# Forgetting heads scored in pairs with the decay summed into the scores, and the relative-position masks moved into the output projection

## The chip, the cores and the metric

The kernel runs on one core of one Trainium2 chip. The metric is the device time of one execution in microseconds (us). Five engines work side by side and wait for each other through semaphores: TensorE (PE in the rows; its weight loads are PEld), VectorE (DVE), ScalarE (ACT), GpSimd (POOL) and SyncE (SP), which issues the transfers from HBM.

## The reference, cut to what matters

Two transformer blocks run one after the other on 256 tokens of width 1024. The change lies in the mixer of the first block. It has three parts side by side: a gated part, six forgetting heads and four heads over a memory of 256 rows. Their outputs are joined and projected by `w_out`.

```
c = jnp.cumsum(log_f, axis=1).transpose(0, 2, 1)
for i in range(S // Q_BLOCK):                 # two blocks of 128 queries
    s = einsum('bhtd,bhsd->bhts', q[block i], k[keys up to the block's end]) * scale
    s = s + c[:, :, start:end, None] - c[:, :, None, :end]
    s = jnp.where(mask, s, NEG_INF)
    p = jax.nn.softmax(s, axis=-1)
    outs.append(einsum('bhts,bhsd->bthd', p, v))
...
y = jnp.concatenate([out_a, out_b, out_c], axis=-1) @ w_out[l]
```

A softmax row doesn't change when one number is added to all of it, so the term of the query, `c[start:end]`, may be left out of `s`; the term of the key may not.

The first attention of the second block adds a bias that depends on the distance of two positions through 32 buckets. The kernel builds it from masks: for each pair of positions, and for each bucket, whether the distance is at or above the bucket's threshold.

## The kernel before, in words

Activations stand with the features on the partitions, two halves of 128 tokens. Weights come from HBM in `raw` tiles; each tile is cut into chunks of up to 1024 columns, and each chunk is split into a high part `wh` (ScalarE, L103) and a low part `wl` (VectorE, L113), so that a product in three passes (high x high, low x high, high x low) keeps float32 precision. `Stream.get` hands out the next chunk and starts the split of the chunk four further on; a low part is issued when the following chunk is split, or by `ws.low()`. The last low part of a `raw` tile lets SP issue the next transfer.

The order on each engine is the order of the code: nothing is moved by a scheduler. `Pipe` interleaves the attention heads with the dense products. Each `step()` scores a head ahead, transposes the probabilities of the head two steps back (L321), runs the masks and the maximum of the newest head (`front`) and the scaling of the head before it (`attn_tail`, L299) on VectorE, and the exponentials on ScalarE. `score` takes two heads together when both say `halves`: their products use 64 rows each of TensorE, on different halves of the rows. Before the change only the memory heads do.

For a forgetting head TensorE makes the scores (L310: 128 queries against 128 keys, then 128 against 256), and in a bank of its own (`pb`) the running sum of minus the log of the gate over the keys (L738, L739), by multiplying a column of `nlf`, spread over 128, with a triangle and a block of ones (`uone`). `decay()` sums the query's term into `ct` (L730 to L732). VectorE adds `pb`, `ct` and the causal mask (L749) and then adds the scores and takes the maximum (L754).

While the heads run, `rel_parts()` prepares the steps of the position bias (18 small VectorE instructions, L564 to L571, on a tile `rbd` that GpSimd clears), and `t5_mask` makes four masks: GpSimd subtracts positions (L578, tile `n`), VectorE compares with the thresholds (L580, tile `o`). GpSimd also masks the gated part's weights `wst` with the triangle (L818) and later scales `gv` (L839).

After the heads comes the output projection: eight chunks of `w_out`, twelve products of 512 columns each (L159 to L161), the last two chunks interleaved bank by bank. Between the third and the fourth chunk `gmlp_out` multiplies the gated part: three times a VectorE instruction `t` (L854), a product `f` on GpSimd (L858) and a split into `oh` (ScalarE) and `ol` (VectorE, L223). Behind the projection TensorE turns the masks into the bias (`t5_mm`, L587) while the norm of `y` is computed.

## Time and profile before

| what | value |
|---|---|
| time, median of 3 runs | 1241.44 us (1239.43 to 1244.65) |
| the profiled execution's own time | 1249.46 us |
| its span, from the first to the last instruction | 1247.7 us |
| TensorE products, busy | 1221.4 us (98%) |
| VectorE, busy | 840.4 us (67%) |
| ScalarE, busy | 658.1 us (53%) |
| GpSimd, busy | 175.6 us (14%) |
| TensorE's mean granted clock | 0.991 of full speed |

Busy shares are means over the whole span; a stage can have another limit. A time after "start us" counts from the span's start. Products are pipelined, and their ends are modelled: what one costs is read from its start to the start of the next. A row that merges several instructions says how many (x2); float32 products appear as two each. The note in brackets at a row's end is the idle time of the engine just before it and what ended that.

### The profile page before, as it was taken

The page shows a single profiled execution, that of the slowest core. Times are in us where ns is not written, and L with a number is a line of the kernel's source. Part 1 is how long each engine was busy: PE and PEld are TensorE (multiplying, and loading weights), DVE is VectorE, ACT ScalarE, POOL GpSimd, SP SyncE. Part 2 cuts the span into 40 slices and gives each one's busy share as a digit, 9 for nine tenths or more (in the row PEclk, how much of TensorE's full clock was granted, in tenths as well). Part 3 has the DMA queues.
Part 4 walks back from the last instruction along what each step waited for, and adds up shares of the span by engine and source line. Part 5 has one row for each costly group of instructions (what it writes and reads, how often), then busy time and mean ns, then how long its engine had stood idle before and what let it go on. Part 6 is the DMA issues. An engine that isn't in the chain of part 4 may idle for free.

```text
span 1247.7 us, 23873 instructions
## 1 busy us (share of the span) xinstructions
PE 1221.4 (98%) x9844; PEld 1165.4 (93%) x9844; DVE 840.4 (67%) x1482; ACT 658.1 (53%) x1164; POOL 175.6 (14%) x169
## 2 busy tenths in 40 slices
PE   8999999999999999999999999999999989999998
PEld 7878899888899999988999999999999869999998
DVE  6786776754578666698666666666666797666553
ACT  5455765443554544577545444445454787545442
POOL 5422200300202001122100001100001462000000
PEclk9799999999999999999999999999999999999999
DMA  7524354655344545532555456545556422555463
GB/s 237 199 89 148 137 199 173 213 196 200 122 152 165 202 144 187 211 136 94 177 185 188 168 166 207 199 173 203 172 168 209 167 68 89 182 184 189 161 203 111
DMA packets 37262, 211.31 MB, mean 169 GB/s; under 512 B 4768, under 2 KB 8224, under 8 KB 18848
## 3 DMA queue, kind: packets, MB, share of 16 engines
q1 hardware_dynamic: 37152, 209.78, 48.6%
q8 instruction: 77, 1.26, 0.4%
q14 instruction: 33, 0.27, 0.1%
HBM read 208.71 MB, written 1.05 MB: 168 GB/s over the span
## 4 chain that ended last, share of the span: by engine, by line
PE 84%; DVE 10%; ACT 3%; issue 2%; DMA 1%; POOL 0%; SPq 0%; ACTq 0%; DVEq 0%
PE ps L135 23%; PE ps L137 23%; PE ps L136 23%; DVE wl L113 3%; PE ps L159 3%; PE ps L161 3%; PE ps L160 3%; PE ps L310 1%; PE ps L342 1%; PE ps L321 1%; DVE p L299 1%; DMA raw<-in_w1q 1%; PE ps L145 1%; PE ps L146 1%; ACT wh L103 1%
## 5 line engine op out<-in xcount | busy, mean ns | idle before, releaser
L113 DVE TENSOR_TENSOR wl<-raw,wh 128x1024 fp32r<-128x1024 f32 (+4 forms) x436 | 491.2, 1165 | 57.1 <-ACT wh L103 56.7
L135 PE MATMUL ps<-xh,wh 128*128 128x256 f32 (+1 forms) x1848 | 522.8, 283 | 2.2 <-DVE y L526 1.7
L137 PE MATMUL ps<-xh,wl 128*128 128x256 f32 (+1 forms) x1848 | 517.6, 280 | 2.5 <-DVE wl L113 2.5
L136 PE MATMUL ps<-xl,wh 128*128 128x256 f32 (+1 forms) x1848 | 518.5, 281 | 0.5 <-DVE xl L271 0.5
L103 ACT CAST wh<-raw 128x1024 fp32r<-128x1024 f32 (+4 forms) x436 | 400.2, 958 | 92.8 <-PE ps L160 37.8
L135 PEld LDWEIGHTS ps<-xh,wh 128*128 128x128 f32 (+1 forms) x1848 | 348.9, 189 | 5.0 <-ACT sq L208 2.1
L137 PEld LDWEIGHTS ps<-xh,wl 128*128 128x128 f32 (+1 forms) x1848 | 348.9, 189 | 3.0 <-DVE wl L113 2.9
L136 PEld LDWEIGHTS ps<-xl,wh 128*128 128x128 f32 (+1 forms) x1848 | 348.9, 189 | 0.9 <-DVE xl L271 0.7
L137 PE MATMUL ps<-ah,wl 128*128 128x256 f32 x704 | 195.7, 278 | 0.0
L136 PE MATMUL ps<-al,wh 128*128 128x256 f32 x704 | 195.4, 278 | 0.0
L135 PE MATMUL ps<-ah,wh 128*128 128x256 f32 x704 | 195.4, 278 | 0.0
L408 ACT ACTIVATE s<-t 128x256 f32<-128x256 f32 x88 | 36.9, 419 | 189.1 <-DVE t L406 189.1
L136 PEld LDWEIGHTS ps<-al,wh 128*128 128x128 f32 x704 | 132.3, 188 | 0.0
L137 PEld LDWEIGHTS ps<-ah,wl 128*128 128x128 f32 x704 | 132.2, 188 | 0.0
L135 PEld LDWEIGHTS ps<-ah,wh 128*128 128x128 f32 x704 | 131.9, 187 | 0.0
L209 POOL TENSOR_TENSOR acc<-acc,sq 128x256 f32<-128x256 f32 x49 | 55.2, 1127 | 516.7 <-ACT sq L208 516.2
L406 DVE TENSOR_TENSOR t<-ps,rb 128x256 f32<-128x256 f32 x88 | 37.2, 422 | 71.6 <-PE ps L137 65.0
L262 ACT ACTIVATE xh<-x,cols 128x256 fp32r<-128x256 f32 x56 | 28.5, 509 | 105.9 <-DVE x L454 94.6
L223 DVE TENSOR_TENSOR al<-f,ah 128x256 fp32r<-128x256 f32 (+1 forms) x104 | 48.8, 470 | 52.5 <-ACT ah L222 52.5
L222 ACT CAST ah<-f 128x256 fp32r<-128x256 f32 (+1 forms) x104 | 45.7, 440 | 56.6 <-DVE f L410 43.2
L410 DVE TENSOR_TENSOR f<-ps,s 128x256 f32<-128x256 f32 x88 | 37.4, 425 | 47.5 <-ACT s L408 47.5
L453 DVE SCALAR_TENSOR_TENSOR t<-ps,rb 128x256 f32<-128x256 f32 x32 | 13.6, 425 | 74.0 <-PE ps L137 74.0
(278 smaller groups left out, 1422.2 us busy)
## 6 DMA issues: line engine op xcount, KB each, us to landing
raw<-in_gu SPq DMA_DIRECT2D x88, 1024.0 KB, 4.8
raw<-in_dn SPq DMA_DIRECT2D x64, 704.0 KB, 4.4
raw<-in_ff SPq DMA_DIRECT2D x32, 1024.0 KB, 4.8
raw<-in_w_out SPq DMA_DIRECT2D x4, 1024.0 KB, 4.8
raw<-in_aq SPq DMA_DIRECT2D x4, 1024.0 KB, 5.0
raw<-in_a_out SPq DMA_DIRECT2D x4, 1024.0 KB, 5.7
raw<-in_b_out SPq DMA_DIRECT2D x4, 1024.0 KB, 5.0
raw<-in_w1q SPq DMA_DIRECT2D x6, 512.0 KB, 4.1
```

Source lines behind the costliest of these rows:

```text
L103: act.copy(h[:, :n], t)
L113: eng.tensor_tensor(out=lo, in0=t, in1=h.bitcast(F32), op=ALU.subtract)
L135: pe.matmul(ps, lhsT=h[:, c:c + m], rhs=x[0][k], start=s0, stop=False)
L136: pe.matmul(ps, lhsT=h[:, c:c + m], rhs=x[1][k], start=False, stop=False)
L137: pe.matmul(ps, lhsT=lo[:, c:c + m], rhs=x[0][k], start=False, stop=s1)
L159: pe.matmul(ps, lhsT=x[0][k][:, ts], rhs=h[:, c:c + n], start=s0, stop=False)
L160: pe.matmul(ps, lhsT=x[1][k][:, ts], rhs=h[:, c:c + n], start=False, stop=False)
L161: pe.matmul(ps, lhsT=x[0][k][:, ts], rhs=lo[:, c:c + n], start=False, stop=s1)
L209: gp.tensor_tensor(out=acc, in0=acc, in1=sq, op=ALU.add)
L222: act.copy(h, src)
L223: dve.tensor_tensor(out=lo, in0=src, in1=h.bitcast(F32), op=ALU.subtract)
L410: dve.tensor_tensor(out=f, in0=u, in1=s, op=ALU.mult)
```

## The change: what it does

1. Forgetting heads are scored two by two (`halves=True`). The decay of the keys is summed by TensorE straight into the scores' bank: `add_fox` follows the scores of each block of queries, with 128 columns for the first block, and 256 and then 128 for the second. The query's term is left out, and with it `decay()`, `ct` and the bank `pb`. VectorE's front is one instruction per block that adds the mask and takes the maximum.
2. `rel_parts()` and the four `t5_mask` leave the heads' steps. `rel_parts()` stands in front of the projection, the masks before its chunks 1, 2, 4 and 5 (counted from 0).
3. The masking of `wst` goes from GpSimd to VectorE, behind the multiplication that gives `km`.
4. The broadcast of the memory norm (`rbm`) goes one dense product later.

```diff
-                pe.matmul(u["ps"][:, o:o + n], lhsT=u["q"][:, i * P:i * P + P], rhs=u["k"][:, :n], start=True, stop=True)
-        for u in us:
-            if "pre" in u:
-                u["pre"](u)
+                pe.matmul(u["ps"][:, o:o + n], lhsT=u["q"][:, i * P:i * P + P], rhs=u["k"][:, :n], start=True, stop="add" not in u)
+            for u in us:
+                if "add" in u:
+                    u["add"](u, i, u["ps"][:, o:o + n])
...
-        def decay():
-            pc = bank()
-            pe.matmul(pc[:, 0:6], lhsT=uone[:, :P], rhs=lf[:, 0], start=True, stop=True)
-            pe.matmul(pc[:, 6:12], lhsT=ones, rhs=lf[:, 0], start=True, stop=False)
-            pe.matmul(pc[:, 6:12], lhsT=uone[:, :P], rhs=lf[:, 1], start=False, stop=True)
-            dve.tensor_copy(ct, pc[:, 0:12])
-
-        def pre_fox(u):
+        def add_fox(u, i, ps):
             h = u["i"]
-            u["pb"] = pb = bank()
-            pe.matmul(pb[:, :T], lhsT=nlf[:, 0, h:h + 1].to_broadcast([P, P]), rhs=uone, start=True, stop=False)
-            pe.matmul(pb[:, P:T], lhsT=nlf[:, 1, h:h + 1].to_broadcast([P, P]), rhs=uone[:, :P], start=False, stop=True)
+            pe.matmul(ps, lhsT=nlf[:, 0, h:h + 1].to_broadcast([P, P]), rhs=uone[:, :P + i * P], start=False, stop=not i)
+            if i:
+                pe.matmul(ps[:, P:T], lhsT=nlf[:, 1, h:h + 1].to_broadcast([P, P]), rhs=uone[:, :P], start=False, stop=True)
...
-            def decayed(i, o, n):
-                return lambda: dve.scalar_tensor_tensor(
-                    out=s[:, o:o + n], in0=pb[:, :n], scalar=ct[:, 6 * i + h:6 * i + h + 1],
-                    in1=cmask[:, o:o + n], op0=ALU.add, op1=ALU.add)
-
-            def scored(i, o, n):
+            def masked(i, o, n):
                 return lambda: dve.tensor_tensor_reduce(
-                    out=s[:, o:o + n], in0=ps[:, o:o + n], in1=s[:, o:o + n], scale=1.0,
+                    out=s[:, o:o + n], in0=ps[:, o:o + n], in1=cmask[:, o:o + n], scale=1.0,
                     scalar=-3e38, op0=ALU.add, op1=ALU.max, accum_out=mx[:, i:i + 1])
...
-            return [decayed(0, 0, P), decayed(1, P, T), scored(0, 0, P), scored(1, P, T),
+            return [masked(0, 0, P), masked(1, P, T),
...
-                          w=(P, T), front=front_fox, pre=pre_fox, o=6 + h))
+                          w=(P, T), front=front_fox, add=add_fox, o=6 + h, halves=True))
...
-            if i == 0:
-                decay()
-            else:
+            if i:
                 _, rs_m = norm_cols(macc)
...
-        rbm = bcast(rs_m, "rbm")
         pipe.step()
         mm_t(pk[:, T:], ws.get(), 0, P, M, range(KT), True, True)
+        rbm = bcast(rs_m, "rbm")
         pipe.step()
         for i in range(2):
             dve.tensor_tensor(out=km[i], in0=pk[:, i * T:i * T + T], in1=rbm, op=ALU.mult)
+        dve.tensor_tensor(out=wst, in0=wst, in1=uone[:, None, :P].to_broadcast([P, 6, P]), op=ALU.mult)
...
-        rel_parts()
-        n5 = mp.tile([P, 2, 8, P], I32, tag="ml", name="n5")
-        o5 = mp.tile([P, 4, 8, P], BF16, tag="mem", name="o5")
...
             pipe.step()
-            t5_mask(c, [n5[:, c % 2]], [o5[:, c]])
         warm_table(AF.Gelu_apprx_tanh)
-        gp.tensor_tensor(out=wst, in0=wst, in1=uone[:, None, :P].to_broadcast([P, 6, P]), op=ALU.mult)
...
+        rel_parts()
+        n5 = mp.tile([P, 2, 8, P], I32, tag="ml", name="n5")
+        o5 = mp.tile([P, 4, 8, P], BF16, tag="mem", name="o5")
         py = [[bank() for _ in range(2)] for _ in range(2)]
         for i, k in enumerate(MIX_ORDER):
+            if i in (1, 2, 4, 5):
+                c = i - 1 - i // 4
+                t5_mask(c, [n5[:, c % 2]], [o5[:, c]])
             if i == 3:
                 gmlp_out()
```

How the order on the engines moves is shown at three places. On TensorE, the scores of the first two forgetting heads before the change (L730 to L732 are `decay`, L310 the scores, L738 and L739 the sums in `pb`):

```order
L730 MATMUL ps<-lf,kon 128x6
L731 MATMUL ps<-lf,kon 128x6
L732 MATMUL ps<-lf,kon 128x6
L310 MATMUL ps<-fk_164,fq_161 128x128
L310 MATMUL ps<-fk_164,fq_161 128x256
L738 MATMUL ps<-kon,nlf 128x256
L739 MATMUL ps<-kon,nlf 128x128
L310 MATMUL ps<-fk_164,fq_161 128x128
L310 MATMUL ps<-fk_164,fq_161 128x256
L738 MATMUL ps<-kon,nlf 128x256
L739 MATMUL ps<-kon,nlf 128x128
```

The same place of the changed kernel (L311 are the scores, L730 and L732 the sums):

```order
L311 MATMUL ps<-fk_164,fq_161 128x128 x2
L730 MATMUL ps<-kon,nlf 128x128 x2
L311 MATMUL ps<-fk_164,fq_161 128x256 x2
L730 MATMUL ps<-kon,nlf 128x256
L732 MATMUL ps<-kon,nlf 128x128
L730 MATMUL ps<-kon,nlf 128x256
L732 MATMUL ps<-kon,nlf 128x128
```

The two heads' products now stand next to each other, with the sums behind each block of queries; `decay` is gone, and two sums of 128 columns are new. On VectorE, the start of the output projection before the change (`ut` is the gated part's input, `t` the first instruction of `gmlp_out`, the two `wl` the low parts of the projection's chunks 4 and 5):

```order
L843 TENSOR_TENSOR ut<-ps,rb 128x256 x3
L113 TENSOR_TENSOR wl_1332<-raw_1135,wh_1331 128x1024
L113 TENSOR_TENSOR wl_1347<-raw_1135,wh_1346 128x1024
L854 SCALAR_TENSOR_TENSOR t<-ps,cols,bsb 128x256
L223 TENSOR_TENSOR ol_188<-f,oh_180 128x256
```

The same place of the changed kernel, from the second of the three rounds of bias steps on (`rbd`, `rt` and `dr` belong to `rel_parts`, `o` is a threshold of a mask; the first round stands in front of these rows):

```order
L572 TENSOR_TENSOR dr<-dr,rt 128x16
L568 CAST rt<-dr 128x16
L570 COPY rbd<-rt 32x16 x4
L581 TENSOR_SCALAR o_1300<-n_1299,cols 128x1024
L113 TENSOR_TENSOR wl_1306<-raw_1089,wh_1305 128x1024
L581 TENSOR_SCALAR o_1300<-n_1299,cols 128x1024
L113 TENSOR_TENSOR wl_1323<-raw_1089,wh_1322 128x1024
L835 SCALAR_TENSOR_TENSOR t<-ps,cols,bsb 128x256
```

The bias steps and two thresholds now stand between the last `ut` and the first `t`. On VectorE again, behind the gated part before the change (the low parts of the projection's last two chunks, then of the next stage's first):

```order
L223 TENSOR_TENSOR ol_190<-f,oh_182 128x256
L113 TENSOR_TENSOR wl_1363<-raw_1234,wh_1362 128x1024
L113 TENSOR_TENSOR wl_1416<-raw_1234,wh_1415 128x1024
L113 TENSOR_TENSOR wl_1432<-raw_1313,wh_1431 128x1024
```

and in the changed kernel:

```order
L223 TENSOR_TENSOR ol_190<-f,oh_182 128x256
L113 TENSOR_TENSOR wl_1341<-raw_1183,wh_1340 128x1024
L581 TENSOR_SCALAR o_1300<-n_1299,cols 128x1024
L113 TENSOR_TENSOR wl_1394<-raw_1183,wh_1393 128x1024
L581 TENSOR_SCALAR o_1300<-n_1299,cols 128x1024
L113 TENSOR_TENSOR wl_1412<-raw_1262,wh_1411 128x1024
```

A threshold stands in front of the last chunk's low part and another behind it; each waits for its subtraction on GpSimd, and GpSimd makes these two subtractions behind the third `f`.

## Rows read from the trace of the kernel before

**Rows 1.** Busy us of PE, PEld, DVE, ACT, POOL by stretch; granted clock, DMA, GB/s.
```profile
41.00:55.00 14.00, 14.00 (x57) 12.09 (x56) 10.32 (x19) 5.72 (x11) 6.20 (x7) 0.51 0.53 173
...
87.00:96.00 9.00, 4.93 (x33) 3.85 (x32) 9.00 (x14) 5.12 (x13) 5.05 (x3) 0.99 0.62 227
...
109.00:133.00 24.00, 24.00 (x120) 19.07 (x120) 13.50 (x19) 13.63 (x23) 2.68 (x4) 1.00 0.40 145
133.00:140.00 7.00, 5.94 (x119) 5.40 (x119) 4.77 (x11) 4.88 (x13) 1.85 (x3) 1.00 0.62 254
```
**Rows 2.** Timeline of TensorE, 86 to 100 us: start, length, instruction, idle time before.
```profile
88.82 0.72 PE L321 MATMUL ps<-kon,p 128*128 128x128 f32 x4 [1.60 <-DVE p L299]
...
95.10 0.72 PE L321 MATMUL ps<-kon,p 128*128 128x128 f32 x4 [2.46 <-DVE p L299]
...
95.89 0.41 PE L137 MATMUL ps<-xh,wl 128*128 128x256 f32 x1
...
99.30 0.28 PE L135 MATMUL ps<-xh,wh 128*128 128x256 f32 x1
```
**Rows 3.** Timeline of VectorE and GpSimd, 90 to 95 us.
```profile
90.33 0.74 DVE L580 TENSOR_SCALAR o<-n,cols 128x1024 bf16<-128x1024 int32 x1
...
91.14 1.90 POOL L578 TENSOR_TENSOR n<-posr,posc 128x1024 int32<-128x1024 int32 x1 [2.75 <-DVE o L580]
...
92.98 2.23 DVE L299 TENSOR_SCALAR p<-p,rd 128x256 f32<-128x256 f32 x2
93.00 1.80 POOL L818 TENSOR_TENSOR wst<-wst,kon 128x768 f32<-128x768 f32 x1
```
**Rows 4.** Timeline of TensorE at the scores of forgetting and memory heads.
```profile
43.55 0.43 PE L730 MATMUL ps<-lf,kon 128*128 128x6 f32 x2
...
44.76 1.65 PE L310 MATMUL ps<-fk,fq 64*128 64x128 f32 x4
...
60.93 0.92 PE L310 MATMUL ps<-fk,fq 64*128 64x128 f32 x4
61.78 0.70 PE L738 MATMUL ps<-kon,nlf 128*128 128x256 f32 x2
62.32 0.38 PE L739 MATMUL ps<-kon,nlf 128*128 128x128 f32 x2
62.54 0.49 PE L321 MATMUL ps<-kon,p 128*128 128x128 f32 x3
...
76.40 1.14 PE L310 MATMUL ps<-km,mq 64*128 64x256 f32 x8
```
**Rows 5.** Timeline of VectorE at the bias steps, and its next instruction.
```profile
76.52 0.17 DVE L564 TENSOR_TENSOR dr<-relb 128x16 f32<-128x16 f32 x1
...
80.88 0.18 DVE L571 TENSOR_TENSOR dr<-dr,rt 128x16 f32<-128x16 f32 x1
...
83.15 0.69 DVE L766 TENSOR_REDUCE mx<-ps 128x2 f32<-128x512 f32 x1
```
**Rows 6.** Timeline of GpSimd and VectorE around the output projection.
```profile
106.83 2.64 POOL L839 TENSOR_TENSOR gv<-gv,vr 128x384 f32<-128x384 f32 x2
...
112.45 2.36 DVE L113 TENSOR_TENSOR wl<-raw,wh 128x1024 fp32r<-128x1024 f32 x2 [1.42 <-ACT wh L103]
118.15 0.48 DVE L854 SCALAR_TENSOR_TENSOR t<-ps,cols,bsb 128x256 f32<-128x256 f32 x1 [3.34 <-PE ps L851]
...
124.67 1.22 DVE L113 TENSOR_TENSOR wl<-raw,wh 128x1024 fp32r<-128x1024 f32 x1
126.78 5.77 DVE L113 TENSOR_TENSOR wl<-raw,wh 128x1024 fp32r<-128x1024 f32 x5 [0.89 <-ACT wh L103]
```
**Rows 7.** Timeline of TensorE, first product with the last chunk's low part.
```profile
128.61 0.39 PE L161 MATMUL ps<-wl,oh 128*128 128x512 f32 x1
```
**Rows 8.** Timeline of GpSimd and VectorE in a later feed-forward stage.
```profile
376.51 2.81 POOL L578 TENSOR_TENSOR n<-posr,posc 128x1024 int32<-128x1024 int32 x1 [32.18 <-DVE o L580]
...
377.49 2.92 DVE L113 TENSOR_TENSOR wl<-raw,wh 128x1024 fp32r<-128x1024 f32 x1
```

## The prediction

> **What bounds the kernel now.** I read the busy time by stretches first. From 109 to 133 us, where the output projection of the first block runs, TensorE is busy for all of the 24.00 us and VectorE for 13.50; from 87 to 96 us, the end of the attention heads, it is the other way round: VectorE is busy for all 9.00 us and TensorE for 4.93 [rows 1]. So TensorE sets the time nearly everywhere, and around 90 us VectorE does. [...]

> Next TensorE's own timeline. Before 88.82 it sat idle for 1.60 us and before 95.10 for 2.46 us, both times for `p`, the probabilities that VectorE scales at L299. Behind the longer wait its products run at the lower clock, from 95.89 to 99.30 (0.41 us long instead of 0.28) [rows 2]. Third, VectorE and GpSimd in that place: the scaling from 92.98 lasts 2.23 us for two instructions, and it ends when GpSimd has ended the masking of `wst` that ran from 93.00 for 1.80 us; a threshold instruction of a mask takes VectorE another 0.74 us, its subtraction on GpSimd 1.90 us [rows 3]. The mask work that shares these steps with the heads is what TensorE waits for.

> **The change, part by part.** Sums are made against the profiled execution's 1249.46 us, 1.76 above its span and 8.02 above the median of 1241.44; the difference that comes out is then applied to the median.

> *Scores.* A forgetting head now costs TensorE 60.93 to 62.54, 1.61 us: the two score products 0.85, the sums 0.54 for 256 columns and 0.22 for 128 [rows 4]. The memory heads are already scored two by two: four products of 256 columns in 1.14 us [rows 4], so 0.57 for two of 256 and half of it, 0.28, for two of 128. For two heads the scores fall from 1.70 to 0.85; the sums grow, because the first 128 keys are summed again for the first half of the queries, from 1.52 to 0.22 x 4 + 0.54 x 2 = 1.96. Saved: 0.41 a pair, 1.2 us for three. If the two products don't overlap once sums stand between them, the scores stay at 1.70 and each pair loses 0.44 (1.3 us for three); I take the overlap, since the two products of a pair still stand next to each other. `decay` took 43.55 to 44.76, 1.21 us at the lower clock; that is work of 0.6 us at the full one, and I count 0.6. Together 1.8 us. VectorE loses two additions a head, which TensorE didn't wait for.

> *Masks and steps taken out of the heads.* Both waits should go, 1.60 + 2.46 = 4.1 us, since neither a threshold nor a GpSimd instruction is left in those steps, and with them the stretch at the lower clock: 3.41 us at half speed lost 1.7 us [rows 2]. Gain so far: 1.8 + 4.1 + 1.7 = 7.6 us.

> *Costed at nothing.* Masking `wst` moves to VectorE, before the fifth head's step. By a low part's 1.22 us for 1024 columns [rows 6] its 768 take some 0.9 us (estimate); VectorE covers it, as that head's scores stand ready a step earlier than before, and uncovered it would cost at most that 0.9. The broadcast for `km` is the same instructions one product later; `km` is first needed two steps on.

> *The same work put into the projection.* Here the order matters. VectorE now does the 18 bias steps, a threshold, a low part of the weights, a threshold and a low part before the first `t` of the gated part, where it had just two low parts. The bias steps took 76.52 to 83.15 = 6.6 us with two subtractions of GpSimd beside them; the second and third of their three rounds, alone, took 2.27 us from 80.88, so 3.4 us for all without GpSimd [rows 5]. In the new place GpSimd ends the scaling of `gv` at 109.47 [rows 6] and goes on to both subtractions at once, so that about one of the two falls on the steps: I take 5.4. With two thresholds (1.5) it is 6.9 us; VectorE's idle time there was 1.42 + 3.34 = 4.8 us [rows 6]. The gated part's chain starts 2.1 us late (0.1 to 3.3 by the two ends).

> Behind that chain GpSimd runs the third and fourth subtraction without a break, beside VectorE's low parts. What such an overlap costs stands later in the trace: a low part of 1024 columns beside a subtraction took 2.92 us instead of 1.22, and the subtraction 2.81 instead of 1.90 [rows 3, 6, 8]. So 1.7 us for each of two, plus the threshold that now stands between the two low parts (0.74), less the 0.89 that VectorE waited there for ScalarE's high part [rows 6]: 3.25 us (from 0, if nothing collides, to 4.1, if the 0.89 stays).

> That makes the low part of the projection's last chunk 2.1 + 3.25 = 5.35 us late. It was done at 126.78 + 1.22 = 128.00, and TensorE took it up at 128.61 [rows 6, 7]: 0.61 us to spare. TensorE waits 4.7 us, in two pieces, one for each of the last two chunks. Queued behind the waiting threshold on VectorE are the low parts of the next stage's first chunks and the norm of `y`: another threshold puts them 6.1 us late at most, about as late as TensorE, so they add nothing. The refills on SP's queue wait for low parts and move with them; they bring chunks of the next stage, with four split chunks in front. After waits of 2.46 us and more the clock fell [rows 2]; I add one such stretch, 1.7 us (0 to 6.9, half of the 13.7 us at the lower level that 14.00 us at a mean of 0.51 amount to [rows 1]). Given back: 4.7 + 1.7 = 6.4 us.

> [...]

> **The sum.** 7.6 gained, 6.4 given back: 1.2 us faster, 1240.2 us.

> **The rivals.**
> *The projection swallows the masks.* For it speaks that VectorE is idle for 10.5 of 24 us there [rows 1]; against it that the idle time lies in front of the gated part and the margin of 0.61 us behind them. With no collision at all the whole 7.6 stays: 1233.8 us. If only the bias steps slip through, with nothing late in front of the chain, TensorE waits 2.6, loses 1.7 by the clock, and 3.3 us stay: 1238.1 us.
> *The clock stays low behind the new wait.* The place is the last two chunks of the projection and the norm of `y` behind them, where TensorE waits again. One stretch of the two seen was four times as long as the other. 13.7 us at half speed cost 6.9 in the place of 1.7: 4.0 us slower, 1245.4 us. From a low stretch of 2 x (7.6 - 4.7) = 5.8 us on the kernel is slower than before. Against it: at the norm itself, from 133 to 140 us, TensorE was idle for 1.06 of 7.00 us and the clock stayed full [rows 1].
> *Scoring two by two doesn't overlap with sums between.* Then the 1.2 us gained on the pairs become 1.3 lost, 2.5 in all: 1.3 us slower than before, 1242.7 us. For it speaks that no pair in this kernel has such sums between its halves.

> **How the numbers follow.** The forecast, with the masks' cost back in the projection, gets 0.50, with its own range of 1237.5 to 1243; the projection swallowing everything 0.13, the bias steps alone 0.12; the long low clock 0.13; no overlap 0.12. A measurement of this kernel can tell about 0.5%, 6.2 us, from no change: faster means below 1235.2, slower above 1247.6. Faster gets the first rival's 0.13 and a little of the forecast's lower side, 0.17; slower gets those cases of the long low clock in which the wait is larger too, 0.06; the same 0.77. The range runs from 1234.0, nearly the swallowed masks, to 1246.0, a little above the long low clock.

> **What would show it.** TensorE without idle time for `p` between 85 and 95 us, and full clock there; a pair of forgetting heads in about 2.8 us from the first score product to the end of the last sum; the projection's first product some 7 us earlier. Then idle time of TensorE before a product with `wl` in the last two chunks, several us, with VectorE in a stretched low part or held threshold and GpSimd in a subtraction at that time; and a fall of the clock behind it. I am wrong if the projection runs without idle time (then 1234), if the waits for `p` stay (then the gain of 5.8 us isn't there), or if the clock takes longer to return than 5.8 us.

## The result and the profile after

The changed kernel takes 1250.52 us (median of 4 runs, 1249.70 to 1250.94), the kernel before 1241.37 in the same comparison: 1.0075 times as long, 95% interval 1.0060 to 1.0091. The forecast was 1240.2 with a range up to 1246.0. It is slower by about 9 us, and the forecast is wrong.

The profiled execution of after took 1250.49 us, like its other runs; that of before took 8 us more than its median. So the two spans (1248.7 and 1247.7 us) hide the loss, and stages have to be compared one by one. First the places of which the prediction spoke: busy time by stretches of after (columns as in [rows 1]).

```profile
85.00:95.00 10.00, 10.00 (x86) 9.27 (x85) 6.30 (x11) 9.29 (x18) 2.02 (x1) 1.00 0.49 179
...
115.00:119.00 4.00, 1.05 (x5) 0.55 (x3) 4.00 (x2) 3.99 (x6) 3.18 (x2) 0.96 0.00 0
119.00:127.00 8.00, 7.53 (x20) 5.50 (x21) 7.27 (x8) 3.92 (x9) 0.00 (x0) 0.59 0.59 208
```

The heads end without a wait and at full clock, where [rows 1, 2] had both. The wait has moved into the output projection, with VectorE busy all the time, and the clock is low behind it. TensorE's timeline there:

```profile
119.31 0.79 PE L161 MATMUL ps<-wl,oh 128*128 128x512 f32 x1 [3.27 <-DVE wl L113]
...
121.11 0.79 PE L161 MATMUL ps<-wl,oh 128*128 128x512 f32 x1 [0.15 <-DVE wl L113]
...
125.54 0.39 PE L159 MATMUL ps<-wh,oh 128*128 128x512 f32 x1
```

and VectorE's and GpSimd's, the answer to [rows 5, 6]:

```profile
99.34 0.71 DVE L565 TENSOR_TENSOR dr<-relb 128x16 f32<-128x16 f32 x1
...
104.98 0.75 DVE L581 TENSOR_SCALAR o<-n,cols 128x1024 bf16<-128x1024 int32 x1
...
112.59 0.42 DVE L223 TENSOR_TENSOR ol<-f,oh 128x256 fp32r<-128x256 f32 x1 [1.36 <-ACT oh L222]
...
114.76 1.66 DVE L223 TENSOR_TENSOR ol<-f,oh 128x256 fp32r<-128x256 f32 x1 [1.36 <-ACT oh L222]
116.35 2.91 DVE L113 TENSOR_TENSOR wl<-raw,wh 128x1024 fp32r<-128x1024 f32 x1
119.19 0.74 DVE L581 TENSOR_SCALAR o<-n,cols 128x1024 bf16<-128x1024 int32 x1
119.85 1.21 DVE L113 TENSOR_TENSOR wl<-raw,wh 128x1024 fp32r<-128x1024 f32 x1
...
98.13 3.75 POOL L579 TENSOR_TENSOR n<-posr,posc 128x1024 int32<-128x1024 int32 x2
...
114.25 3.93 POOL L579 TENSOR_TENSOR n<-posr,posc 128x1024 int32<-128x1024 int32 x2
```

All this is the mechanism of the forecast in the projection, nearly at its sizes. The 9 us lie elsewhere, where the diff changes no instruction. In each of the four down projections (528 products `ah`, `al` with `wh`, `wl`, 256 columns, no idle time, full clock) I counted TensorE's instructions in 50 us. The rows are the stretch, its length, PE's busy time (instructions), granted clock and DMA. Of before, the first and the last down projection:

```profile
458.00:508.00 50.00, 50.00 (x427) 1.00 0.56 185
...
1188.00:1238.00 50.00, 50.00 (x443) 1.00 0.58 191
```

and of after, the last, and the first feed-forward block's second product (`ff2`, 512 columns):

```profile
1190.00:1240.00 50.00, 50.00 (x419) 1.00 0.51 166
...
240.00:290.00 50.00, 50.00 (x222) 1.00 0.62 223
```

443, 427 or 419 products in the same time: a product every 113.3, 117.8 or 120.0 ns, start to start (a count holds two or three at the edges more than 50 us by the pace). Exactly, from the first and the last product of after's last down projection,

```profile
1181.35 0.29 PE L135 MATMUL ps<-ah,wh 128*128 128x256 f32 x1
...
1244.59 0.28 PE L137 MATMUL ps<-ah,wl 128*128 128x256 f32 x1
```

63.24 us for 527 steps, 120.0 ns. Before ran its four at 117.8, 117.8, 113.3 and 113.3, after all four at 120.0: 528 x (2 x 2.2 + 2 x 6.7) ns = 9.4 us. `ff2` goes the other way, 226.7 ns in place of 233.3: 384 x 6.6 ns = 2.5 us less.

### The profile page after: what moved, and what is told of

The parts are those of the page before. It is cut to its first block, busy times and chain, and to the rows that moved or that the text cites. A ratio compares the mean times of both kernels' runs of the same rounds, so it can differ in the third digit from the quotient of the medians.

```text
span 1248.7 us, 23875 instructions
## 1 busy us (share of the span) xinstructions
PE 1222.7 (98%) x9850; PEld 1169.1 (94%) x9850; DVE 836.3 (67%) x1470; ACT 658.8 (53%) x1164; POOL 171.6 (14%) x168
## 3 DMA queue, kind: packets, MB, share of 16 engines
HBM read 208.71 MB, written 1.05 MB: 168 GB/s over the span
## 4 chain that ended last, share of the span: by engine, by line
PE 84%; DVE 10%; ACT 3%; issue 1%; DMA 1%; POOL 1%; SPq 0%; ACTq 0%; DVEq 0%; POOLq 0%
PE ps L135 23%; PE ps L136 23%; PE ps L137 23%; DVE wl L113 4%; PE ps L161 3%; PE ps L159 3%; PE ps L160 3%; PE ps L343 1%; PE ps L311 1%; PE ps L145 1%; PE ps L147 1%; PE ps L322 1%; PE ps L146 1%; ACT wh L103 1%; DVE p L299 1%
## 5 line engine op out<-in xcount | busy, mean ns | idle before, releaser
L135 PE MATMUL ps<-ah,wh 128*128 128x256 f32 x704 | 199.2, 283 | 0.0
L136 PE MATMUL ps<-al,wh 128*128 128x256 f32 x704 | 199.2, 283 | 0.0
L137 PE MATMUL ps<-ah,wl 128*128 128x256 f32 x704 | 199.2, 283 | 0.0
L137 PEld LDWEIGHTS ps<-ah,wl 128*128 128x128 f32 x704 | 135.2, 192 | 0.0
L136 PEld LDWEIGHTS ps<-al,wh 128*128 128x128 f32 x704 | 135.1, 192 | 0.0
L135 PEld LDWEIGHTS ps<-ah,wh 128*128 128x128 f32 x704 | 135.1, 192 | 0.0
```

Source lines behind the costliest of these rows:

```text
L135: pe.matmul(ps, lhsT=h[:, c:c + m], rhs=x[0][k], start=s0, stop=False)
L136: pe.matmul(ps, lhsT=h[:, c:c + m], rhs=x[1][k], start=False, stop=False)
L137: pe.matmul(ps, lhsT=lo[:, c:c + m], rhs=x[0][k], start=False, stop=s1)
```

## The experiments

**Theories.** A product has a stationary operand (`lhsT` in the code, the 128x128 that PEld loads in the trace) and a moving one (`rhs`); in the products of 256 columns the weights are stationary and the activations move, in `ff2` it is the other way round. Without `ct` (48 bytes, 64 with padding) all SBUF tiles allocated behind it stand 64 bytes lower. In the built program `ah` and `al` start 32 bytes behind a multiple of 128 before and 96 behind one after; the weights start at 96 and `xh`, `xl` at 0 in both. *Address theory*: the pace of a product hangs on where its operands start. Rivals: *order* (the moved instructions leave something behind), *banks* (seven PSUM banks fewer shift the rotation of all later ones). Each run below has 3 or 5 rounds against the kernel before; the ratio is to that.

**Put the 64 bytes back, nothing else.**

```diff
+        ct = sm.tile([P, 12], F32, tag="ct", name="ct")
         smem = sm.tile([P, 2], F32, tag="smem", name="smem")
```

> The changed kernel with the small tile ct put back at its old place, used by nothing: every SBUF tile allocated behind it returns to its address of before (64 bytes up). Address theory: the products of the four down projections follow each other at 113 to 118 ns again instead of 120, which returns about 9 us there, and the second feed-forward product of the first block, which had gained 2.5 us, loses them: 1250.5 - 9.3 + 2.5 = about 1243.7 us (1241 to 1246). Order theory (the moved instructions carry a lasting effect): 1250 us, 120 ns in all four. Bank theory (seven PSUM banks fewer shift the rotation of the banks): 1250 us as well.

1239.21 us, ratio 0.9977 (0.9963 to 0.9992). All four down projections run at 113.3 ns, here the second:

```profile
714.00:764.00 50.00, 50.00 (x444) 1.00 0.58 194
```

**Take the 64 bytes from the kernel before, nothing else.** `ct` goes into a tile that exists already.

```diff
-        ct = sm.tile([P, 12], F32, tag="ct", name="ct")
+        ct = sm.tile([P, 2, 6], F32, tag="nz", name="ct").rearrange("p a b -> p (a b)")
```

> The kernel before, with ct stored in a tile that is already there and free by then (nz), and nothing else changed: every SBUF tile allocated behind it moves 64 bytes down, as the change moves them. Address theory: 120 ns in the four down projections, about 7 us slower than before, 1248 us (1245 to 1250). Order theory and bank theory: no change, 1241.4 us, 113 to 118 ns.

1250.30 us, ratio 1.0072 (1.0046 to 1.0098): the loss of the whole change, with none of its instructions. The last down projection:

```profile
1190.00:1240.00 50.00, 50.00 (x419) 1.00 0.51 165
```

**Restore the bank numbers.**

```diff
+        for _ in range(7):
+            bank()
         y_ = mp.tile([P, 2, D], F32, tag="mh", name="y")
```

> The changed kernel with seven PSUM banks taken and not used ahead of the output projection, so that every later product finds the bank number of before. Bank theory: back to 113 to 118 ns in the down projections, 1243.7 us. Address theory and order theory: no change, 1250.5 us.

1250.14 us, 1.0069 (1.0043 to 1.0095), 120.0 ns. Order and banks are out; the addresses stand in both directions.

**Other addresses.** First 32 bytes in the place of `ct` (`ct` of `[P, 8]`).

> The changed kernel with an unused tile of 32 bytes in the place of ct: every SBUF tile allocated behind it moves 32 bytes up, so that the activations ah and al start at a multiple of 128 bytes (before: 32 behind one, after: 96 behind one). Address theory: another pace than 120 ns in the down projections; if a start at 128 bytes is the good one, 113 ns or less in all four and about 1240 us, otherwise up to 1250. Order theory and bank theory: 1250.5 us.

1245.06 us, 1.0026 (1.0009 to 1.0043): the down projections at 116.7 ns. A start at a multiple of 128 isn't the good one. Then `fill`, a padding ahead of `xh`, from `[P, 8]` to `[P, 16]`, with `ct` of `[P, 8]`:

> The changed kernel with two unused paddings of 32 bytes, one ahead of the activations xh and xl, one in the place of ct: xh and xl now start 32 bytes behind a multiple of 128 (so far at one), and ah and al 32 behind one, as before the change. If the pace hangs on where the moving operand starts, whatever the stage, the some 5470 products of the gate, up and first feed-forward stages go from 117 ns to the 113.3 of the down projections: 5470 x 3.7 ns = 20 us, so 1239.2 - 20 = 1219 us (1215 to 1224). If it is something that only the down projections have, they stay at 117 ns and the time at 1239 us.

1251.03 us, 1.0084 (1.0069 to 1.0098). Neither: with `xh` at 32 the gate and up stages run at 117.8 ns, and the down projections, at the very addresses of before, are at 117.8 in all four. So one pair of addresses has two paces, and which one a stage takes is looked at further down. Then the weights alone (`mhalf` from `[P, 24]` to `[P, 40]`, `fill` to `[P, 24]`):

> The changed kernel with the weight tiles wh and wl moved 64 bytes against everything else: they start 32 behind a multiple of 128 in place of 96, while ah and al stay at 96 and xh and xl at 0. If the distance between the two operands of a product decides (in the kernel before it was 64 bytes in the down projections, here again), the down projections run at 113.3 ns and the time is about 1250.5 - 14 = 1236.5 us. If the moving operand's own start decides, they stay at 120 ns and the time at 1250.5 us.

1262.21 us, 1.0179 (1.0163 to 1.0195). The down projections leave 120.0 though `ah` hasn't moved against 128, so its own start doesn't decide; but they come to 117.8, not 113.3, and the gate and up stages go to 120.0. Rows of a down projection and a gate and up stage, first of e4_plus32, then of e5_both32, then of e6_weights_moved:

```profile
455.00:505.00 50.00, 50.00 (x431) 1.00 0.57 196
...
620.00:670.00 50.00, 50.00 (x431) 1.00 0.54 190
```
```profile
455.00:505.00 50.00, 50.00 (x427) 1.00 0.61 199
...
620.00:670.00 50.00, 50.00 (x427) 1.00 0.53 190
```
```profile
455.00:505.00 50.00, 50.00 (x427) 1.00 0.56 181
...
620.00:670.00 50.00, 50.00 (x419) 1.00 0.53 187
```

**The masks of the mixer, at the addresses of before.** Both edits are made to e1_tile_back. First `rel_parts()` and the masks back in the heads:

```diff
         pg = [bank(), bank()]
+        rel_parts()
...
             pipe.step()
+            t5_mask(c, [n5[:, c % 2]], [o5[:, c]])
```

> The changed kernel with ct's place kept (e1_tile_back, 1239.2 us) and the bias steps and the four masks back in the heads' steps, where they stood before the change. By the prediction's steps the waits for p come back in part (4.1 us and 1.7 of clock for both, less what the masking of wst on GpSimd had in them), and the projection's wait of 3.2 us and the low clock behind it go: 1238 to 1242 us, that is within 3 us of e1_tile_back. Rival: the waits for p don't return since VectorE has two additions a head less; then 1239.2 - 3.2 - 1 = 1235 us.

1237.00 us, 0.9971 (0.9958 to 0.9984), an interval that overlaps that of e1_tile_back. Two waits for `p` come back, 1.33 + 0.84 = 2.2 us where before had 1.60 + 2.46 [rows 2], and the projection runs through:

```profile
83.48 0.72 PE L322 MATMUL ps<-kon,p 128*128 128x128 f32 x4 [1.33 <-DVE p L299]
...
88.13 0.72 PE L322 MATMUL ps<-kon,p 128*128 128x128 f32 x4 [0.84 <-DVE p L299]
...
100.00:124.00 24.00, 24.00 (x122) 19.05 (x119) 14.25 (x19) 13.67 (x23) 4.73 (x5) 1.00 0.41 139
```

Then masks in the projection, but without GpSimd:

```diff
-                t5_mask(c, [n5[:, c % 2]], [o5[:, c]])
+                dve.scalar_tensor_tensor(out=o5[:, c], in0=posr[:, None, :P].to_broadcast([P, 8, P]), scalar=cols[:, C_THR:C_THR + 1],
+                                         in1=posc[:, 8 * c:8 * c + 8, None].to_broadcast([P, 8, P]), op0=ALU.subtract, op1=ALU.is_ge)
```

> e1_tile_back (1239.2 us) with each of the four masks of the mixer made by a single VectorE instruction (position minus threshold, compared with the other position) in place of a subtraction on GpSimd and a threshold on VectorE; the computation is the same. Prediction's theory (a subtraction beside a low part stretches both, and delays the last low part): the low part stands at 1.2 us, TensorE's wait of 2.85 us in the last two chunks falls under 1 us and the clock stays up: 1235 to 1237 us. Rival (VectorE's total work is what is late, and the new instruction is longer than a threshold by itself): the wait stays at about 3 us, 1239 us.

1235.69 us, 0.9968 (0.9957 to 0.9979). The low parts stand at 1.22 us, although the mask instruction is longer (1.28 in place of 0.74), the bias steps take 3.44 us in place of 5.64, and one wait of 0.40 us is left:

```profile
113.57 1.22 DVE L113 TENSOR_TENSOR wl<-raw,wh 128x1024 fp32r<-128x1024 f32 x1
114.70 1.28 DVE L855 SCALAR_TENSOR_TENSOR o<-posr,cols,posc 128x1024 bf16<-128x1024 int32 x1
...
117.17 0.50 PE L161 MATMUL ps<-wl,oh 128*128 128x512 f32 x1 [0.40 <-DVE wl L113]
```

So the collision with GpSimd made the wait, not VectorE's total work. The times of e1, e7 and e8 overlap in their intervals, but the traces show a gain over e1. From the projection's first product to the first product of the next dense stage (`xh` with `wh`), here in before, then in after, then in e8:

```profile
108.84 0.50 PE L159 MATMUL ps<-wh,oh 128*128 128x512 f32 x1
...
138.34 0.35 PE L135 MATMUL ps<-xh,wh 128*128 128x256 f32 x1 [0.86 <-DVE y L526]
```
```profile
97.24 0.50 PE L159 MATMUL ps<-wh,oh 128*128 128x512 f32 x1
...
132.91 0.36 PE L135 MATMUL ps<-xh,wh 128*128 128x256 f32 x1 [0.86 <-DVE y L527]
```
```profile
96.84 0.50 PE L159 MATMUL ps<-wh,oh 128*128 128x512 f32 x1
...
127.36 0.36 PE L135 MATMUL ps<-xh,wh 128*128 128x256 f32 x1 [0.86 <-DVE y L527]
```

That is 29.50, 35.67 and 30.52 us. The six kernels that have the masks with GpSimd there (after, e1, e3 to e6) lie between 34.23 and 36.27, the seven that have the single instruction (e8 to e14) between 30.52 and 30.56: the single instruction saves at least 3.7 us in this stretch.

**Addresses, continued** (all from e8_one_instr). 64 bytes ahead of `ah` in the first feed-forward block alone:

> e8_one_instr (1235.7 us) with an unused tile of 64 bytes ahead of ah and al in the first feed-forward block alone: there, and nowhere else, they start 96 bytes behind a multiple of 128, as in the changed kernel. Address theory: the 384 products of the second feed-forward product take 227 ns in place of 233, 2.5 us less, and the down projections stay as they are: 1233.2 us (1231.5 to 1235). Rival: the pace of that stage has another cause; then 1235.7 us.

1234.98 us, 0.9947 (0.9927 to 0.9966), faster than both kernels, but not for the reason expected: `ff2` runs at 232.4 ns, not at 226.7; the profiled execution had 113.3 in all four down projections, that of e8_one_instr 117.8 in two. Then all operands at a multiple of 128 (`mhalf` `[P, 32]`, no `fill`, `ct` `[P, 8]`):

> e8_one_instr (1235.7 us) with all operands of the dense products (wh, wl, xh, xl, ah, al, oh, ol) starting at a multiple of 128 bytes. If the distance of the two operands decides (0 went with 120 ns in the changed kernel's down projections), all products of 256 columns run at 120 ns: 5470 x 3.3 + 2110 x 4.5 ns = 28 us more, less 2.5 us in the second feed-forward product: about 1261 us (1255 to 1265). If a start at a multiple of 128 is what makes a product fast, they run at 113.3 ns or less: 5470 x 3.4 ns = 18.6 us less and some 5 us in the down projections: about 1212 us.

1260.87 us, 1.0158 (1.0138 to 1.0178), where the distance of the two operands forecast 1261. A down projection and a gate and up stage:

```profile
455.00:505.00 50.00, 50.00 (x419) 1.00 0.58 193
...
620.00:670.00 50.00, 50.00 (x419) 1.00 0.53 182
```

**What picks 113.3 or 117.8.** Two kernels with `xh` and `xl` at 32, except the first of their eight tiles:

> e8_one_instr (1235.7 us) with xh and xl 32 behind a multiple of 128, as in e5_both32, but the first of the eight tiles of each at 96. In e5_both32 all products stayed at 117.8 ns, the slower of two paces seen with 32 and weights at 96 (113.3 is the other), and in the changed kernel the 117.8 ns never stood behind a stage at 96. Theory that one product at 96 brings the faster pace back: (7 x 113.3 + 120) / 8 = 114.1 ns in the gate and up stages, 5470 x 2.9 ns = 16 us less: about 1220 us. Rival: the 117.8 ns stays: about 1243 us.

> The same with the first of the eight tiles at a multiple of 128 in place of 96. In e1_tile_back the 113.3 ns of the down projections stood behind products at a multiple of 128 that ran at 116.7. Theory that one such product keeps the faster pace: (7 x 113.3 + 116.7) / 8 = 113.7 ns, 5470 x 3.3 ns = 18 us less: about 1218 us. Rival: 117.8 ns, about 1243 us.

1247.26 us (1.0047, 1.0028 to 1.0065) and 1247.49 us (1.0051, 1.0034 to 1.0068): 117.8 ns nearly throughout, both theories fell. Then only `xl`, or only `xh`, at 32:

> e8_one_instr (1235.7 us) with only the low parts xl 32 bytes behind a multiple of 128, xh at one as in the kernel before. Theory that products at a multiple of 128 in the stream bring and keep the faster of the two paces: one product in three at 113.3 ns, two at 116.7, on the mean 115.6 in the gate and up stages: 5470 x 1.1 ns = 6 us less, about 1230 us. Rival: 117.8 ns throughout: 1247 us, as in e12_mixed0.

> The same the other way round: xh 32 behind a multiple of 128, xl at one. Two products in three at 113.3 ns, on the mean 114.4: 5470 x 2.3 ns = 12.5 us less, about 1223 us; by the rival 117.8 ns throughout: 1247 us.

1236.20 us (0.9938, 0.9914 to 0.9963) and 1243.17 us (1.0005, 0.9983 to 1.0027). The gate and up stages ran at 117.8 in both, against the theory. Of the down projections, which the expectation left out, e13 ran all four at 113.3 in the profiled execution, e14 one. Rows of e13_low32, a down projection and a gate and up stage:

```profile
448.00:498.00 50.00, 50.00 (x444) 1.00 0.62 213
...
610.00:660.00 50.00, 50.00 (x427) 1.00 0.54 190
```

Last, the kernel before once more:

> The kernel before, unchanged, profiled a second time. Its first profile had 117.8 ns in the first two down projections and 113.3 in the last two. If the pace of a stage is drawn anew in every execution, the stages that run at 117.8 are others here, with 2.3 us for each in the time; if the program sets it, they are the same two.

1242.04 us, 0.9994. The second down projection, at 117.8 ns in the first profile, ran at 113.3; the first, third and fourth as they did. So the program doesn't set the pace of a stage. That the execution does, and not the chip, is borne out by e8: its profiled execution, with two down projections at 117.8, took 1239.75 us, the other eight on the same chip 1234.84 to 1237.25. The rows of e15 for the first and second down projection, and for the stretch from 41 to 55 us:

```profile
455.00:505.00 50.00, 50.00 (x427) 1.00 0.58 194
722.00:772.00 50.00, 50.00 (x444) 1.00 0.61 211
...
41.00:55.00 14.00, 13.55 (x101) 12.18 (x100) 13.86 (x32) 5.97 (x15) 7.78 (x9) 1.00 0.51 171
```

The long low clock of [rows 1] in that stretch was one execution's own as well: 0.51 there, 1.00 here.

## Why the prediction was wrong

**The step that failed** is the removal of `decay()` and `ct`: it was counted as work saved (0.6 us), not as space given up, and the sum took for granted that all behind the norm of `y` runs as before. 64 bytes less moved `ah` and `al` against the weights. From e1_tile_back to after the down projections lose 528 x 4 x 6.7 ns = 14.1 us and `ff2` gains 2.5; that makes 11.6, and the medians differ by 11.3. No rival had this, and the 0.06 for slower stood on a longer low clock only. With the 64 bytes back the time is 1239.21 us, 1.0 below the forecast. That nearness is partly luck: the forecast gain is 1.2 us, and the pace of a single down projection moves the time by 2.3.

**The terms of the sum, as measured.**
- *Waits for `p`*, 4.1 us and the low clock behind them (0.50 from 95.90 to 99.30 us of before): gone, as forecast, but not for the reason given alone. With the masks back in the heads, e7 has 2.2 us of them. So about 1.9 us went by the other edits, such as the two additions a head less (of which the prediction said that TensorE didn't wait for them) and the masking of `wst` away from GpSimd; no run separates these. And the low clock behind the waits isn't sure: e15 had it (0.81 from 87 to 96 us), e2, with waits of 1.50 and 2.48 us, didn't (1.00).
- *`decay`*: 0.6 us forecast, from its 1.21 us at a granted clock of 0.50 (43 to 45 us of before); nothing in the execution of after. There the scores wait 1.22 us for `fk` (the row of 44.41 in the next item). In e15, at full clock, `decay` ran in that time, and 0.45 us of the wait was left over:

```profile
44.36 0.92 PE L310 MATMUL ps<-fk,fq 64*128 64x128 f32 x4 [0.45 <-DVE fk L720]
```

  The scores began at 44.41 in after and at 44.36 in e15. Where the clock was low just before, as in e1 (0.66 from 41 to 46 us), the wait isn't there.
- *Scores two by two*: 0.41 us a pair forecast, 0.2 measured. The first pair lasts from 44.41 to the next product at 47.43, 3.02 us; two single heads took 2 x 1.61 [rows 4]. The sums cost 1.97 as forecast; the scores 0.42 + 0.63 = 1.05 in place of 0.85, so the overlap is there, but not whole:

```profile
44.41 0.49 PE L311 MATMUL ps<-fk,fq 64*128 64x128 f32 x4 [1.22 <-DVE fk L720]
44.83 0.71 PE L730 MATMUL ps<-kon,nlf 128*128 128x128 f32 x4
45.47 0.70 PE L311 MATMUL ps<-fk,fq 64*128 64x256 f32 x4
46.10 0.70 PE L730 MATMUL ps<-kon,nlf 128*128 128x256 f32 x2
...
47.43 0.37 PE L135 MATMUL ps<-xh,wh 128*128 128x256 f32 x1
```

- *Bias steps beside two subtractions*: 5.4 us forecast, 104.98 - 99.34 = 5.64 measured; GpSimd's share as taken, and 3.4 without GpSimd as well (3.44 in e8).
- *The gated part's chain*: 2.1 us late forecast, 2.2 measured. The first `t` began 0.72 us behind the gated part's first product (L851 and [rows 6]) and begins 2.95 behind it in after:

```profile
117.43 1.58 PE L851 MATMUL ps<-wst,gv 128*64 128x128 f32 x24
```
```profile
105.63 1.58 PE L832 MATMUL ps<-wst,gv 128*64 128x128 f32 x24
...
108.58 0.48 DVE L835 SCALAR_TENSOR_TENSOR t<-ps,cols,bsb 128x256 f32<-128x256 f32 x1
```

- *Collision in the last chunks*: 3.25 us forecast. Measured 1.24 on the last `ol` (1.66 in place of 0.42) and 1.70 on the low part (2.91 in place of 1.21), with the threshold's 0.66 and less the 0.89 that is gone: 2.7. I had both subtractions fall on low parts; one fell on `ol`. And GpSimd was hardly slowed, 3.93 for two where two of [rows 3] make 3.80, while [rows 8] had 2.81 for one. The ends show where the time went. In after the first of the two subtractions ended at 114.25 + 1.90 = 116.15 and the `ol` beside it at 116.42, the second at 118.18 and the low part at 119.26: 0.27 and 1.08 us behind, where `ol` took 0.42 and a low part 1.21 with GpSimd idle. In [rows 8] the subtraction at 376.51 began behind another low part:

```profile
376.35 1.22 DVE L113 TENSOR_TENSOR wl<-raw,wh 128x1024 fp32r<-128x1024 f32 x1
```

  That low part ended at 377.57, the subtraction at 379.32, 1.75 behind it (1.90 long in [rows 3]), and the next low part, begun at 377.49, at 380.41, 1.09 behind the subtraction. So in these four cases the instruction that began second ended that length, less 0.13 to 0.15 us, behind the one that had begun first, while the first subtraction in after kept its 1.90. The prediction had read [rows 8] as a pair by itself. What holds the second one up isn't shown.
- *TensorE's wait*: 4.7 us forecast, 3.27 + 0.15 = 3.4 measured. *Low clock behind it*: 1.7 forecast; 13 steps from 119.31 to 125.54, at a granted clock of 0.50, took 6.23 us where 0.23 each, as from 125.54 on at 1.00, would make 3.0, so 3.1 without the 0.15. Together 6.5 for 6.4. The two misses belong together: the three products between the two waits took 1.65 us at the lower clock in place of 0.7, and filled about 1 us of what would have been a wait. How long the clock stays low differs: from 119 to 127 us it is 0.59 in after and 0.57 in e3, but 0.79 to 0.81 in e1, e4, e5 and e6, a loss of some 1.7 us as forecast.

The totals mix all this with the pace of the down projections. Two stretches of the mixer, in us, don't: the heads, from the last dense product ahead of the first scores to the projection's first product, and the projection, from there to the first product of the next dense stage (one execution of each kernel; the low clock in it differs).

| stretch | before, e15, e2 | after | e1, e3 to e6 | e7 | e8 to e14 |
|---|---|---|---|---|---|
| heads | 65.51 (long low clock), 61.02, 59.09 | 54.33 | 52.86 to 54.14 | 55.74 | 53.21 to 54.41 |
| projection | 29.50, 29.51, 28.94 | 35.67 | 34.23 to 36.27 | 29.50 | 30.52 to 30.56 |

From e15 or e2 to after the heads gain 6.7 or 4.8 us (7.6 forecast) and the projection gives back 6.2 or 6.7 (6.4 forecast). So the price of the move was right, the gain nearly so, and whether a net gain is left can't be told from these stretches; e1_tile_back is 0.2% faster in its time. But e7, with the masks in their old place, keeps most of the gain of the heads and pays nothing in the projection: moving masks that GpSimd subtracts brought 1 to 3 us and cost 5 to 7. With the single instruction the move costs 1.

## What to carry to other kernels

A deleted tile moves everything allocated behind it: compare the start addresses of the operands of the long product stages before and after, and keep the place with an unused tile while testing an edit. When a time changes and no wait explains it, count instructions per 50 us in stages that the diff doesn't touch, and compare start to start, since the length of one product (0.28 us in all cases here) shows nothing. A profile that lies 8 us off its own median isn't one to subtract another from.

## What the runs showed of the hardware

For float32 products of 256 columns, at full clock and without a wait, start to start:

| stationary start, mod 128 | moving start, mod 128 | distance, mod 128 | ns | seen in |
|---|---|---|---|---|
| 96 | 96 | 0 | 120.0 | down projections of after, e2, e3 |
| 0 | 0 | 0 | 120.0 | all such stages of e10 |
| 32 | 0 | 32 | 120.0 | gate and up of e6 |
| 96 | 32 | 64 | 113.3 or 117.8 | down projections of before, e1, e5 (117.8), e7, e8, e9, e11 and e12 (117.8), e13 to e15; gate and up of e5 (117.8) |
| 32 | 96 | 64 | 117.8 | down projections of e6 |
| 96 | 0 | 96 | 116.7 or 117.8 | gate and up of before, after, e1; down projections of e4 (116.7) |
